# First stage with a fixed issue order and fp32 conditioning rows in column groups, and the second layer's output weights split early and kept in DRAM

## Chip, cores and metric

One core of one Trainium2 chip runs the whole program in one launch. The metric is the device time of an execution in microseconds (us); the median of several runs is compared.

## The reference, cut to what matters

Two layers over 2048 latent tokens of width 1024 and 256 context tokens. All arrays are fp32. Each layer computes

```python
shift, scale, gate = split(silu(c) @ w_mod + b_mod, 3)      # one row per stream (latent, context)
hx = rmsnorm(x, g_pre) * (1 + scale) + shift
q, k, v, ga, uf, gf, zc, bc, cc, gc = split_cols(hx @ w_in)
a = window_attention(rope(q), rope(k), v, kc, vc, sink)     # window 128 and 256 context keys
f = fourier_mix(uf, w_fourier)                              # 2-D FFT, then a 64x64 product per group
s = short_conv_mix(zc, bc, cc, conv_w, conv_b)
y = concat(a * silu(ga), f * silu(gf), s * silu(gc)) @ w_out
x = x + gate * rmsnorm(y, g_post)
```

The first product, `silu(c) @ w_mod`, is called the conditioning rows here: the columns for `shift` and `scale` of layer 0 (2048 of them, for the two streams) must be known before any token can be projected, and their weights are 8 MB.

## The kernel before

A large product is computed from two rounded parts of each operand: `split` (L76) writes `hi`, the fp32r rounding of the source, and `lo`, the rounded rest. It takes two letters, the engine for `hi` and the one for `lo`: v is VectorE, a ScalarE, p GpSimd. `proj_k` (L309) is then three matmuls, hi*hi, hi*lo and lo*hi, over 512 tokens. PE is TensorE.

Each layer has three parts: `half` (L782) for tokens 0 to 1023 and then for 1024 to 2047, each in two chunks of 512 tokens, projects all columns and writes q, k, v, the gates and the mixer inputs to DRAM; `phase2` (L1313) runs over blocks of 128 tokens: scores and softmax (`u_qk`, letter A), the product with the values (`u_pv`, B) and the output projection (`u_out`, C), interleaved by order strings such as `ORDER_1`. In `half` small generators ("fills") are advanced by `tick` after each `proj_k`, at a rate from `RT` or `FF`; a fill goes on at each yield.

Every DMA of the kernel is issued by SyncE (SP) in one queue, in order. The framework schedules the instructions of each engine in the order that its own planner finds, unless an instruction is kept in program order (`keep_in_program_order`) or put behind another (`issue_after`, in the kernel `behind`).

- `startup` (L652) is the first stage. It loads in the order of the string `LD` (g: a 512 KB tile of conditioning weights, x: 128 tokens of x, w: two tiles of projection weights, b: biases) and works in the order of `START`. `mod_mm(g)` (L685) makes a quarter of the conditioning rows: 8 weight slices of 128x512, each split in two (`MSH`, `MSL`), each part multiplied with a 4-column stationary operand (both streams, hi and lo), 16 matmuls for a quarter and 64 in all; then a copy, four transposes, a sum, and bias and gain. Letter m is one slice (the ninth m of a quarter its end), p one of eight `p0_post` steps (four transposes of x, scale and shift on ScalarE, split), W a weight split, 0 to 3 a `proj_k` of one of the four blocks of 128 columns, r the squares for chunk 1 (`pt_r`), y the steps of chunk 1 (`pt_row`, `pt_post`). A quarter serves two of the eight p steps. Chunk 1 of the same four blocks and the context tokens follow in `half` from L881 on, then `form_b` (L399).
- `tab_gen` (L612) is a fill of layer 0, half 0: it loads a piece of the FFT table, splits it (`a`, `v`) and stores it to `ftd`.
- `fft_b` (L543) is a fill of half 1 in both layers. Its tables come through `tab`, three buffers `ftb`. After the first split it yields four times before the first matmuls `pf`.
- `wout_gen` (L1280) makes the output weights in `phase2`: eight tiles of 512 KB are loaded and split there, in its first four steps (letters V and W of `ORDER_0` to `ORDER_3B`), into the four `big` buffers; those of W become free when the last `late` projection (L1054) is done.
- In `u_pv` (L1157) the half of the mixer output that doesn't come from attention (`fct`, by DMA) is split on GpSimd at the key tile t = 1 into `hfh` and `hfl`.

Of the kernel before, what the change touches and what calls it, by code (L numbers as in the profile page):

```python
# [16 lines left out]
DEPTH = 2  # L17
# [15 lines left out]
WE_B = ["vv", "vp", "vv", "av"]  # L33
WV_A = ["vv", "av", "vv", "vv"]
WV_B = ["vv", "av", "vv", "av"]
# [3 lines left out]
ORDER_3A = "bAAWCCBcBCABBAWCBBCBBCcACBCBB"  # L39
ORDER_3B = "bAAWCCBcBCABBAWCBBCBBCcACBCBB"  # L40
# [3 lines left out]
WST = ["ap", "av", "av", "vv"]  # L44
# [20 lines left out]
class Kern:  # L65
# [10 lines left out]
    def split(self, hi, lo, src, hi_eng="v", lo_eng="v"):  # L76
        nc = self.nc
        if hi_eng == "v":
            self.last_v = nc.vector.tensor_copy(hi, src)  # L79
        elif hi_eng == "a":  # L80
            nc.scalar.activation(hi, src, AF.Copy, bias=0.0, scale=1.0)  # L81
        else:
            nc.gpsimd.tensor_scalar(hi, src, 1.0, 1.0, op0=ALU.mult, op1=ALU.mult)  # L83
        if lo_eng == "v":
            self.last_v = nc.vector.tensor_tensor(lo, src, f(hi), op=ALU.subtract)  # L85
        else:
            nc.gpsimd.tensor_tensor(lo, src, f(hi), op=ALU.subtract)  # L87
# [136 lines left out]
    def p0_pre(self, l, base, n, ctx, xt, load=True, eng=None, sq=()):  # L224
# [14 lines left out]
        for i in range(nt):  # L239
            if eng and eng[i] == "p":  # L240
# [7 lines left out]
    def p0_post(self, l, ps, tag, xt, h, n, ctx, lo_eng="vpvpvpvp"):  # L248
# [4 lines left out]
        for k in range(KT):  # L253
            pt = ps.tile([128, CH], F32, name="pt", tag=tag)
            for i in range(n // 128):
                nc.tensor.transpose(pt[:, i * 128:(i + 1) * 128], xt[i][:, k * 128:(k + 1) * 128], self.ident)
            t = self.xp.tile([128, CH], F32, name="ht", tag="ht", bufs=2)
            nc.scalar.activation(t[:, :n], pt[:, :n], AF.Identity, bias=S[:, k, s:s + 1], scale=G[:, k, s:s + 1])
# [3 lines left out]
    def pt_r(self, slot, base, n, ctx, xt=None):  # L262
# [6 lines left out]
        for i in range(nt):  # L269
            jk = self.xp.tile([128, D], BF16, name="jk", tag="jk", bufs=1)  # L270
            self.last_sq = nc.scalar.activation(jk, xt[i], AF.Square, bias=0.0, scale=1.0,
                                                accum_out=ssq[:, i:i + 1])
# [9 lines left out]
    def pt_row(self, slot, n, ps, rb):  # L282
# [7 lines left out]
        nc.scalar.copy(rb, pb[:, :n])  # L290
        return rb

    def pt_post(self, T, h, n, ctx):
# [5 lines left out]
        for k in range(KT):  # L299
            u = self.xp.tile([128, CH], F32, name="ht", tag="ht", bufs=2)[:, :n]  # L300
            nc.vector.scalar_tensor_tensor(u, T[k], G[:, k, s:s + 1], rb, op0=ALU.mult, op1=ALU.mult)
            nc.scalar.activation(hi[:, k, :n], u, AF.Identity, bias=S[:, k, s:s + 1], scale=1.0)
            nc.vector.scalar_tensor_tensor(lo[:, k, :n], u, S[:, k, s:s + 1], f(hi[:, k, :n]), op0=ALU.add, op1=ALU.subtract)
# [5 lines left out]
    def proj_k(self, a, W, h, n, k):  # L309
# [3 lines left out]
        nc.tensor.matmul(a, wh[:, k, :], hi[:, k, :n], start=(k == 0), stop=False)  # L313
        nc.tensor.matmul(a, wh[:, k, :], lo[:, k, :n], start=False, stop=False)  # L314
        nc.tensor.matmul(a, wl[:, k, :], hi[:, k, :n], start=False, stop=(k == KT - 1))  # L315
# [227 lines left out]
    def fft_b(self, fp, ps, AB, ct):  # L543
# [42 lines left out]
        for _ in range(4):  # L586
            yield
# [24 lines left out]
    def tab_gen(self, p):  # L612
        nc = self.nc
        for k in range(9):
            raw = p.tile([128, 384], F32, name="tr", tag="tr")
            nc.sync.dma_start(raw, self.I["ftab"][:, k])
# [4 lines left out]
            yield  # L621
# [30 lines left out]
    def startup(self, ps, hx, blocks, st, wps, gps):  # L652
# [5 lines left out]
        slots = [t[:, i] for t in tmp for i in range(2)]  # L658
        slots += [st.tile([128, D], F32, name=n, tag=n) for n in ("cosT", "sinT")]
        slots += [gps.tile([128, D], F32, name=f"wmg{i}") for i in range(2)]  # L660
        wm = [big[k // 4][:, k % 4] for k in range(KT)] + slots

        def load(i):
            nc.sync.dma_start(wm[i], self.I["wmod0"][i])

        cs = gps.tile([128, KT, 4], F32R, name="cshl")
        self.split(cs[:, :, 0::2], cs[:, :, 1::2], self.cs, "v", "v")
        n = {"g": 0, "x": 0, "w": 0, "b": 0}
        for c in LD:
# [6 lines left out]
            elif c == "w":  # L676
                raws = [self.wraw(self.I["wina"][0, j]) for j, _ in blocks[:2]]
            else:
# [4 lines left out]
        post = self.p0_post(0, ps, "tr", x0, hx, CH, False)  # L683

        def mod_mm(g):  # L685
            pr = ps.tile([4, CH], F32, name="pmr", tag="fft")
            for k in range(KT):
                tags = (("qh", "ql"), ("rt", "rs"))[k % 2]
                hi, lo = [st.tile([128, CH], F32R, name=f"w{t}", tag=t, bufs=2) for t in tags]
                self.split(hi, lo, wm[4 * g + k // 2][:, k % 2 * CH:(k % 2 + 1) * CH], MSH[8 * g + k], MSL[8 * g + k])  # L690
                nc.tensor.matmul(pr, cs[:, k, :], hi, start=(k == 0), stop=False)
                nc.tensor.matmul(pr, cs[:, k, :], lo, start=False, stop=(k == KT - 1))
                yield
            row = st.tile([128, CH], F32, name="sg", tag="sg", bufs=2)[:4]
            nc.scalar.copy(row, pr)
            pc = ps.tile([128, 2, 2, 2, 2], F32, name="pmc", tag="fft")
            for n in range(2):
                for i in range(2):
                    o = (2 * n + i) * 128
                    nc.tensor.transpose(pc[:, n, i], row[:, o:o + 128], self.ident[:4, :4])  # L700
            sm = gps.tile([128, 2, 2, 2], F32, name="msum", tag="msum")
            nc.vector.tensor_reduce(sm, pc, axis=mybir.AxisListType.X, op=ALU.add)
# [845 lines left out]
```

## Time and profile before

| | us |
|---|---|
| median of 3 runs | 2036.09 (2033.15 to 2039.77) |
| profiled execution, device time | 2036.74 |
| its span in the profile | 2034.9 |
| PE busy in it | 1973.3 (97%) |
| VectorE / ScalarE / GpSimd busy | 1242.0 / 848.6 / 753.6 |

The span is the time from the first to the last recorded instruction; the device time is 1.8 us longer. A matmul's recorded duration is longer than its share of PE, since matmuls overlap: the distance of two starts is what one costs. "Idle before" is time in which the engine had nothing running, with the work that released it. Of the 40 slices of the span PE is at 6 tenths in the first, at 9 or more in the 38 after it, and at 8 in the last.

### The profile page before, as it was taken

How to read it: one execution, taken by the hardware profiler on the slowest of the kernel's cores; microseconds unless marked ns; L12 is line 12 of the kernel's file. 1: busy time of each engine (PE TensorE's matmuls, PEld its weight loads, DVE VectorE, ACT ScalarE, POOL GpSimd, SP SyncE). 2: the span in 40 equal slices, each digit the busy share in tenths (PEclk: the TensorE clock that was granted, in tenths of full speed). 3: DMA queues.
4: the chain of work that ended last, by engine and by line, in shares of the span. 5: the costliest groups of instructions: out<-in, count | busy, mean ns of one | idle time of the engine just before them, and what ended most of it. 6: DMA issues, size and time to landing. Idle time of an engine off the chain costs nothing. (4 is left out here: it accounts for less than half of the span.)

```text
span 2034.9 us, 28515 instructions
## 1 busy us (share of the span) xinstructions
PE 1973.3 (97%) x10232; PEld 1670.6 (82%) x10232; DVE 1242.0 (61%) x2239; ACT 848.6 (42%) x1742; POOL 753.6 (37%) x965
## 2 busy tenths in 40 slices
PE   6999999999999999999999999999999999999998
PEld 2898878897887788888877988889788778888886
DVE  7825695646525677777768323142754377777775
ACT  6522212313224556666666322131222356666663
POOL 4322212305342444444455233242234334444442
PEclk8999999999999999999999999999999999999999
DMA  7775654466467344443334533134554834444321
GB/s 298 226 250 158 206 185 141 142 199 186 158 168 218 96 112 115 114 115 104 127 122 137 164 96 94 62 119 132 156 168 141 239 109 116 114 116 113 110 63 42
DMA packets 187038, 291.63 MB, mean 143 GB/s; under 512 B 15608, under 2 KB 119696, under 8 KB 185872
## 3 DMA queue, kind: packets, MB, share of 16 engines
q1 hardware_dynamic: 186896, 289.80, 47.2%
q8 instruction: 81, 1.33, 0.3%
q14 instruction: 61, 0.50, 0.1%
HBM read 214.37 MB, written 75.38 MB: 142 GB/s over the span
## 5 line engine op out<-in xcount | busy, mean ns | idle before, releaser
L315 PE MATMUL acc<-big,wl 128*128 128x512 f32 x1152 | 452.4, 393 | 5.5 <-DVE wl L85 2.9
L313 PE MATMUL acc<-big,wh 128*128 128x512 f32 x1152 | 455.7, 396 | 1.4 <-DVE wh L79 1.4
L314 PE MATMUL acc<-big,wh 128*128 128x512 f32 x1152 | 451.3, 392 | 0.0
L87 POOL TENSOR_TENSOR wl<-wr,wh 128x1024 fp32r<-128x1024 f32 x63 | 162.9, 2586 | 377.4 <-ACT wh L81 234.9
L85 DVE TENSOR_TENSOR pl<-tp,ph 128x512 fp32r<-128x512 f32 x320 | 219.0, 687 | 105.6 <-ACT ph L81 101.2
L1141 ACT ACTIVATE pt<-pt,nm 128x640 f32<-128x640 f32 (+2 forms) x272 | 216.2, 795 | 130.2 <-DVE nm L1138 129.7
L315 PEld LDWEIGHTS acc<-big,wl 128*128 128x128 f32 x1152 | 217.9, 189 | 53.1 <-DVE wl L85 4.2
L313 PEld LDWEIGHTS acc<-big,wh 128*128 128x128 f32 x1152 | 218.5, 190 | 43.8 <-ACT czc L991 1.5
L314 PEld LDWEIGHTS acc<-big,wh 128*128 128x128 f32 x1152 | 218.1, 189 | 42.4 <-DVE big L85 0.2
L81 ACT ACTIVATE ph<-tp 128x512 fp32r<-128x512 f32 x320 | 188.8, 592 | 131.6 <-PE tp L1179 122.1
L1138 DVE CUSTOM_DVE_ANT_0 pt<-sp,mask,nsink 128x640 f32<-128x640 f32 (+2 forms) x256 | 213.3, 841 | 20.7 <-PE sp L1128 15.0
L1153 POOL TENSOR_SCALAR pt<-pt,rv 128x640 f32<-128x640 f32 (+2 forms) x272 | 213.2, 804 | 26.9 <-DVE rv L1151 26.1
L1179 PE MATMUL tp<-ident,pt 128*128 128x128 f32 x1280 | 197.1, 275 | 10.1 <-POOL pt L1153 9.5
L1179 PEld LDWEIGHTS tp<-ident,pt 128*128 128x128 f32 x1280 | 160.1, 141 | 56.8 <-POOL pt L1153 15.3
L358 POOL TENSOR_TENSOR rs<-rs,sinT 128x512 f32<-128x512 f32 x40 | 66.0, 1653 | 170.0 <-DVE rs L356 165.2
L1131 PE MATMUL sp<-kseg,qt 128*128 128x384 f32 (+1 forms) x512 | 128.6, 331 | 0.0
L1228 PE MATMUL yp<-big,hfh 128*128 128x512 f32 x272 | 118.7, 436 | 1.0 <-POOL hfh L83 1.0
L1146 POOL TENSOR_TENSOR es<-nm,nsink 128x4 f32<-128x4 f32 x68 | 14.5, 214 | 283.2 <-DVE nm L1138 283.2
L1228 PE MATMUL yp<-big,hah 128*128 128x512 f32 x272 | 117.1, 431 | 0.1
L1128 PE MATMUL sp<-kctx,qt 128*128 128x256 f32 x544 | 114.2, 292 | 2.9 <-DVE nm L1138 2.0
L1128 PEld LDWEIGHTS sp<-kctx,qt 128*128 128x128 f32 x544 | 95.6, 189 | 16.4 <-DVE nm L1138 3.5
L1230 PE MATMUL yp<-big,hfl 128*128 128x512 f32 x272 | 108.1, 397 | 0.5 <-POOL hfl L87 0.4
(382 smaller groups left out, 3807.9 us busy)
## 6 DMA issues: line engine op xcount, KB each, us to landing
wr<-in_wina SPq DMA_DIRECT2D x76, 512.0 KB, 3.6
qt<-qs SPq DMA_DIRECT2D x34, 512.0 KB, 4.7
wmt<-in_wmodt SPq DMA_DIRECT2D x32, 512.0 KB, 4.3
ftb<-ftd SPq DMA_DIRECT2D x36, 384.0 KB, 3.7
xt<-in_x SPq DMA_DIRECT2D x26, 512.0 KB, 5.8
kseg<-ks SPq DMA_DIRECT2D x24, 512.0 KB, 7.9
xt<-x SPq DMA_DIRECT2D x24, 512.0 KB, 5.1
gat<-gas SPq DMA_DIRECT2D x34, 256.0 KB, 3.1
```

The lines of the kernel that those rows point to most:

```text
L81: nc.scalar.activation(hi, src, AF.Copy, bias=0.0, scale=1.0)
L85: self.last_v = nc.vector.tensor_tensor(lo, src, f(hi), op=ALU.subtract)
L87: nc.gpsimd.tensor_tensor(lo, src, f(hi), op=ALU.subtract)
L313: nc.tensor.matmul(a, wh[:, k, :], hi[:, k, :n], start=(k == 0), stop=False)
L314: nc.tensor.matmul(a, wh[:, k, :], lo[:, k, :n], start=False, stop=False)
L315: nc.tensor.matmul(a, wl[:, k, :], hi[:, k, :n], start=False, stop=(k == KT - 1))
L1128: nc.tensor.matmul(sp[:, 256:512], B.q[:, h, :], self.kctx[:, kv, x, :], start=(x == 0), stop=(x == 1))
L1138: self.last_m = nc.vector.tensor_tensor_reduce(d, x, m, scale=-0.125, scalar=self.nsink[:, h:h + 1], op0=ALU.add, op1=ALU.min, accum_out=n ...
L1141: self.last_x = nc.scalar.activation(pt, pt, AF.Exp, bias=nm[:, hh:hh + 1], scale=-1.0, accum_out=sm[:, hh:hh + 1])
L1153: self.last_p = nc.gpsimd.tensor_scalar(B.pts[kv][g], B.pts[kv][g], rv[:, g:g + 1], 1.0, op0=ALU.mult, op1=ALU.mult)
L1179: nc.tensor.transpose(tp[:, hh * 128:(hh + 1) * 128], pts[hh][:, t * 128:(t + 1) * 128], self.ident)
L1228: nc.tensor.matmul(yp, hh, wh[:, k, :], start=(i == 0), stop=False)
```

## The change

1. First stage. Every instruction of it goes through `self.kp`, which keeps it in program order while `START` runs. The conditioning weights are no longer split: a slice is one fp32 matmul with a 32-column stationary operand (two columns are used), and slices k go in turn to the four column groups 0, 32, 64 and 96, whose results lie in four groups of 32 rows and are summed after the transposes. A step m is now two slices, and a quarter has five steps. `LD`, `START` and the engines of several small steps are new: x is loaded first, all four weight blocks and the x of chunk 1 in the same queue; nine steps i at the start are four transposes of the identity each; the scaling of x goes from GpSimd to ScalarE and VectorE, the low parts of p from half GpSimd to all VectorE, all four W to ScalarE and VectorE.
2. Layer 1's output weights are split by a new fill, `wout_split`, in half 0 of layer 1 (16 pieces of 128x512) and stored to DRAM (`wos`); `phase2` of layer 1 loads both parts, twice the bytes, with no split there. The first block of a layer splits `fct` at its last key tile (of layer 0's first block this is t = 1 as before).
3. `tab_gen` loads a piece ahead, and `fft_b` yields once, not four times, after its first split.
4. Evacuations of chunk 0 are put behind the copy of the row factors (`last_rb`), the context's row factors are made one k later, and `form_b_w` of later halves is put behind `last_v`.

```diff
-LD = "gggxgxxxgggwbggggggggg"
-XE = "pppv"
-START = "mmmmmmmmmmmWmpp0m1mm1m00mp1pmm0mmmW123p32mmmmp0m1m2m13m03mm2rmm3pp102y23y001213yyyyy01y23"
+LD = "xxxxgbgggwcggggggggggggX"
+XE = "avav"
+START = "iiiiiiiiimmmmWmpp00W11WWmmmmm2233ppmmmm00m112233ppmmmm00mr1122pp330011y2233yzyyy"
-RT = 0.6, 0.594, 0.616, 0.1, 0.15, 0.12, 0.49, 0.16
+RT = 0.6, 0.594, 0.616, 0.1, 0.15, 0.12, 0.49, 0.16, 0.27
+ORDER_2B = "bAACACACCCBCBCBCBABBCBBB"
+ORDER_3B = "bWAAWCCBcBCABBAWCBBCBBCcACBWCBB"
...
         def mod_mm(g):
-            pr = ps.tile([4, CH], F32, name="pmr", tag="fft")
+            pr = ps.tile([128, CH], F32, name="pmr", tag="fft")
             for k in range(KT):
-                tags = (("qh", "ql"), ("rt", "rs"))[k % 2]
-                hi, lo = [st.tile([128, CH], F32R, name=f"w{t}", tag=t, bufs=2) for t in tags]
-                self.split(hi, lo, wm[4 * g + k // 2][:, k % 2 * CH:(k % 2 + 1) * CH], MSH[8 * g + k], MSL[8 * g + k])
-                nc.tensor.matmul(pr, cs[:, k, :], hi, start=(k == 0), stop=False)
-                nc.tensor.matmul(pr, cs[:, k, :], lo, start=False, stop=(k == KT - 1))
-                yield
+                q = 32 * (k % 4)
+                self.kp(nc.tensor.matmul(pr[q:q + 32], cs[:, k, :], wm[4 * g + k // 2][k % 2],
+                                         start=(k < 4), stop=(k >= 4), tile_position=(0, q)))
+                if k % 2:
+                    yield
...
+            elif c == "i":
+                w = ps.tile([128, CH], F32, name="warm", tag="tr")
+                for i in range(4):
+                    self.kp(nc.tensor.transpose(w[:, i * 128:(i + 1) * 128], self.ident, self.ident))
...
         h = part(0)
-        for _ in range(4):
-            yield
+        yield
...
+        raw = load(0)
         for k in range(9):
-            raw = p.tile([128, 384], F32, name="tr", tag="tr")
-            nc.sync.dma_start(raw, self.I["ftab"][:, k])
+            yield
+            nx = load(k + 1) if k < 8 else None
             yield
...
+            elif half == 0:
+                fills.append(self.start_fill(self.wout_split(l, self.pool(e3, "wop", bufs=1)), RT[8]))
...
-            if kv == 1 and t == 1:
+            if kv == 1 and t == (1 if B is not self.Bs[0] else nkt - 1):
...
+    def wout_load(self, l, n):
+        W = [self.big(), self.big()]
+        self.wout.append(W)
+        for c in (2, 3, 0, 1):
+            with self.behind(self.last_st):
+                for t, src in zip(W, self.wos[n]):
+                    self.nc.sync.dma_start(f(t[:, 2 * c:2 * c + 2]), src[:, 2 * c:2 * c + 2])
+            yield
+
+    def wout_split(self, l, p):
+        nc = self.nc
+
+        def load(i):
+            t = p.tile([128, CH], F32, name="wo", tag="wo", bufs=2)
+            nc.sync.dma_start(t, self.I["woutk"][l, i // KT, :, i % KT])
+            return t
+
+        raw = load(0)
+        for i in range(2 * KT):
+            yield
+            nx = load(i + 1) if i + 1 < 2 * KT else None
+            yield
+            h = p.tile([128, 2, CH], F32R, name="wh2", tag="wh2", bufs=2)
+            self.split(h[:, 0], h[:, 1], raw, "a", "v")
+            nc.sync.dma_start(self.wos[i // KT, :, :, i % KT].rearrange("x p c -> p x c"), f(h))
+            raw = nx
+        yield
```

## Rows read from the trace of the kernel before

**Rows 1.** Busy time in stretches of 50 us: PE, PEld, DVE, ACT, POOL, clock, DMA.
```profile
250.00:300.00 50.00, 46.09 (x231) 39.02 (x230) 42.85 (x73) 8.42 (x16) 11.72 (x5) 0.97 0.65 216
...
450.00:500.00 50.00, 45.66 (x213) 37.86 (x213) 36.95 (x80) 14.39 (x25) 22.27 (x14) 0.97 0.56 156
...
1450.00:1500.00 50.00, 45.83 (x227) 38.72 (x226) 31.35 (x52) 16.47 (x30) 25.76 (x18) 0.97 0.75 205
...
1600.00:1650.00 50.00, 45.38 (x233) 37.04 (x232) 35.85 (x61) 25.31 (x53) 17.86 (x21) 0.97 0.62 200
...
sum 2050.00, PE 1973.31 PEld 1670.56 DVE 1241.95 ACT 848.59 POOL 753.55; mean PE 48.13 PEld 40.75 DVE 30.29 ACT 20.70 POOL 18.38
```

**Rows 2.** PE in order of time, 0 to 40 us: start, duration, idle before.
```profile
6.08 0.59 PE L691 MATMUL pmr<-wqh,cshl 128*4 128x512 f32 x1 [6.08 <-ACT wqh L81]
...
21.11 0.48 PE L256 MATMUL pt<-ident,xt 128*128 128x128 f32 x1 [3.71 <-POOL xt L241]
```

**Rows 3.** Groups by line, 0 to 62 us: busy us, mean ns, idle before.
```profile
L691 PE MATMUL pmr<-wqh,cshl 128*4 128x512 f32 x16 | 7.4, 461 | 8.4 <-ACT wqh L81 8.4
...
L271 ACT ACTIVATE jk<-xq 128x1024 bf16<-128x1024 f32 x4 | 4.2, 1054 | 0.1
...
L695 ACT COPY sg<-pmr 4x512 f32<-4x512 f32 x4 | 2.3, 572 | 1.8 <-PE pmr L692 1.7
```

**Rows 4.** Busy time in stretches of 10 us; clock, DMA share and GB/s last.
```profile
0.00:10.00 10.00, 3.67 (x8) 0.55 (x9) 3.31 (x7) 5.32 (x9) 1.82 (x6) 1.00 0.71 277
10.00:20.00 10.00, 3.58 (x14) 0.88 (x12) 2.80 (x6) 8.04 (x15) 4.45 (x8) 0.84 1.02 409
20.00:30.00 10.00, 7.63 (x23) 3.63 (x24) 10.00 (x15) 4.85 (x7) 7.90 (x4) 0.50 1.04 404
30.00:40.00 10.00, 8.50 (x41) 4.93 (x40) 9.15 (x19) 6.57 (x13) 3.48 (x3) 0.98 0.98 390
```

**Rows 5.** PE in order of time, 60 to 93 us.
```profile
60.44 0.60 PE L256 MATMUL pt<-ident,xt 128*128 128x128 f32 x4
60.79 0.48 PE L313 MATMUL acc<-big,wh 128*128 128x512 f32 x1
...
82.75 0.30 PE L289 MATMUL prb<-ident,ht 128*128 128x128 f32 x1 [1.69 <-DVE ht L288]
...
92.57 0.39 PE L315 MATMUL acc<-big,wpl 128*128 128x512 f32 x1
92.80 0.28 PE L313 MATMUL acc<-cxh,wh 128*128 128x256 f32 x1
```

**Rows 6.** PE in order of time, 146 to 148 us: four fp32 products, then a projection.
```profile
146.34 1.05 PE L437 MATMUL pa<-wf,cf 128*128 128x128 f32 x8
147.15 0.48 PE L313 MATMUL acc<-big,wh 128*128 128x512 f32 x1
```

**Rows 7.** VectorE, then PE, in order of time, 288 to 294 us.
```profile
288.51 0.56 DVE L85 TENSOR_TENSOR th<-tr,th 128x384 fp32r<-128x384 f32 x1 [1.54 <-ACT th L81]
...
293.58 0.80 PE L315 MATMUL acc<-big,wl 128*128 128x512 f32 x1 [2.54 <-POOL wl L87]
```

**Rows 8.** SP's queue, then PE, in order of time, 480 to 487 us.
```profile
482.34 0.59 SPq L343 DMA_DIRECT2D qs<-ql  x1
483.03 1.02 SPq L555 DMA_DIRECT2D ftb<-ftd  x2
...
486.38 0.98 PE L428 MATMUL pf<-ftb,fh 128*128 128x256 f32 x6 [3.09 <-DMA ftb<-ftd]
```

**Rows 9.** GpSimd, VectorE and PE in order of time, 1613 to 1642 us.
```profile
1613.52 0.62 POOL L83 TENSOR_SCALAR hfh<-fct 128x512 fp32r<-128x512 f32 x1 [3.07 <-DMA fct<-fs]
...
1637.31 3.23 POOL L87 TENSOR_TENSOR big<-wr,big 128x1024 fp32r<-128x1024 f32 x1 [1.29 <-PE tp L1179]
...
1638.23 2.87 DVE L1070 SCALAR_TENSOR_TENSOR lt<-ht,lt 128x512 f32<-128x512 f32 x1
...
1641.75 0.80 PE L1193 MATMUL op<-pl,vtl 128*128 128x512 f32 x1 [2.24 <-DVE pl L85]
```

More of the change, by code (lines that the diff above doesn't have):

```diff
@@ L289, in pt_row @@
             nc.tensor.transpose(pb[:, sl], w[:, sl], self.ident)
-        nc.scalar.copy(rb, pb[:, :n])
+        self.last_rb = nc.scalar.copy(rb, pb[:, :n])
         return rb
@@ L657, in startup @@
         tmp = [t.rearrange("p k c -> p (k c)").rearrange("p (h c) -> p h c", h=2) for t in tmp]
[L658 to L661, printed above, removed]
-        def load(i):
[L664 to L668, printed above, removed]
+        wm = [big[k // 4][:, k % 4] for k in range(KT)] + [t[:, i] for t in tmp for i in range(2)]
+        wm = [[w[:, i * CH:(i + 1) * CH] for i in range(2)] for w in wm]
+        wm += [[st.tile([128, CH], F32, name=f"w{t}{i}", tag=t, bufs=2) for i in range(2)] for t in ("qh", "ql")]
+        slots = [gps.tile([128, D], F32, name=f"wmg{i}") for i in range(2)]
+        wm += [[w[:, i * CH:(i + 1) * CH] for i in range(2)] for w in slots]
+        craw = [st.tile([128, KT, 128], F32, name=n, tag=n) for n in ("cosT", "sinT")]
+        def load(i):
+            if 12 <= i < 14:
+                for h in range(2):
+                    nc.sync.dma_start(wm[i][h], self.I["wmod0"][i][:, h * CH:(h + 1) * CH])
+            else:
+                t = slots[i - 14] if i >= 14 else (big[i // 4][:, i % 4] if i < 8 else tmp[(i - 8) // 2][:, i % 2])
+                nc.sync.dma_start(t, self.I["wmod0"][i])
+        cs = gps.tile([128, KT, 32], F32, name="cs32")
+        nc.vector.memset(cs, 0.0)
+        nc.vector.tensor_copy(cs[:, :, 0:2], self.cs)
+        n = dict.fromkeys("gxwbcX", 0)
         for c in LD:
@@ L677, in startup @@
                 raws = [self.wraw(self.I["wina"][0, j]) for j, _ in blocks[:2]]
+            elif c == "c":
+                for t, (j, _) in zip(craw, blocks[2:]):
+                    nc.sync.dma_start(t, self.I["wina"][0, j].rearrange("p (k c) -> p k c", k=KT))
+            elif c == "X":
+                self.p0_load(0, CH, CH, False, self.x1)
             else:
@@ L876, in half @@
             if first:
-                self.pt_r(2, 0, NCTX, True, self.xs)
                 _, n, ctx, tok, rp = chunks[0]
-                for (j, ev), acc in zip(blocks0, accs):
-                    ev(acc, n, ctx, tok, rp)
+                with self.behind(self.last_rb):
+                    for (j, ev), acc in zip(blocks0, accs):
+                        ev(acc, n, ctx, tok, rp)
                 h, n, ctx, tok, rp = chunks[1]
@@ L889, in half @@
                         self.proj_k(accs[i], Ws0[i], h, n, k)
-                        if i == 2 and k:
+                        if i == 2 and k > 1:
                             next(pc)
+                            if 4 < k < 7:
+                                next(pc)
                             if k == KT - 1:
@@ L923, in half @@
                 fetch(J_K)
-                WB = self.form_b_w(l, wb)
+                with self.behind(self.last_v):
+                    WB = self.form_b_w(l, wb)
                 if l == 0:
```

108 lines of the change are left out of this document (56 added, 52 removed).

## The prediction

> **What bounds the kernel now.** I read the busy time in stretches of 50 us first. PE is busy for 1973 of 2035 us [rows 1], and its work hardly changes, so a change can gain only what PE loses: 61.6 us without work, and stretches at half clock. The stretches show where. The first 40 us hold 16.6 us of idle PE (6.3, 6.4, 2.4 and 1.5 in turn), with a clock of 0.50, the 1.2 GHz level, from 20 to 30 us [rows 4]. Four later stretches hold 3.9, 4.3, 4.2 and 4.6 us, each with a mean clock of 0.97 [rows 1]; 0.97 over 50 us is 3 us at half clock, so some 1.5 us more is lost in each.
>
> Then the order of time on PE. The first matmul starts at 6.08 us, released by a ScalarE rounding of conditioning weights, and at 21.11 PE stands 3.71 us for GpSimd, which scales x [rows 2]. By line, the first matmul of a slice, hi, waits 8.4 us in all for ScalarE's rounding [rows 3]: the splits feed PE too slowly, while DMA runs at full share and some 400 GB/s [rows 4]. From 60 us on PE is dense but for 1.69 us at 82.75; a projection matmul starts every 0.23 us, and chunk 1 ends at 92.80 us [rows 5]. Chunk 1 is 96 matmuls, at 0.228 us 21.9 us; with the gap it began at 92.8 - 21.9 - 1.7 = 69.2 us. This 69.2 is what the first stage has to beat.
>
> **The change part by part.**
>
> *Conditioning rows.* Removed: 64 matmuls at 0.23, 14.7 us of PE at full clock, and 64 split instructions on three engines. Added: 32 fp32 matmuls of 512 columns. No row shows one in a column group. The nearest are four fp32 products of 128 columns at full width: eight records in 0.81 us (146.34 to 147.15) [rows 6], so each is two records of 0.10 us, 0.203 us in all. Scaled to 512 columns that is 0.81 us, two records of 0.4. Bounds: 0.81 us each with no overlap between column groups, 26 us in all; a quarter of it, 0.2, if four groups run together, 6.5 us. I take the middle, 0.41: the two records of one product use the same columns and cannot overlap, and matmuls start in order, so the first record of the next group can overlap only with the second of the last. That is 13 us, about what is removed. So the gain here is not PE work: it is that nothing stands between a landed tile and its matmul.
>
> The Trainium skill, "TensorE: Matmul & The Clock Gate", Part 3, has three column groups of 32 running 2.38 times as fast as one after the other; no row here shows that. By it the 32 would cost 26/2.38 = 11 us, 2 us less than my sum; with four groups wholly together it is the second case below. "TensorEngine Tiling", Key Properties, speaks against the change: switching the tiling mode drains the engine. The order string switches eight times; with a drain taken as a matmul's recorded 0.39 less its distance of 0.23 [rows 5], that estimate is 1.3 us.
>
> *The first stage anew.* Transfers: x (2.1 MB), 16 conditioning tiles (8.4) and four weight blocks (2.1) come in one queue; 2.8 MB land by 10 us, then about 0.405 MB per us [rows 4]. So quarter 1 is complete after 8.4 MB, at 10 + 5.6/0.405 = 23.9 us, and the last quarter after 12.6 MB, at 34.2. By 23.9 PE can have done quarter 0 and blocks 0 and 1 for k = 0 and 1. After it, in the pinned order, PE has: the last step of quarter 1 and two quarters more, 18 matmuls at 0.41 = 7.4 us; 84 projection matmuls at 0.228 = 19.2 us; six p steps at 0.35 (60.44 to 60.79 [rows 5]) = 2.1 us; three groups of four transposes, 1.1 us. Sum 29.8 us, to 53.7. Waits on top: the end of quarter 1 stands behind its copy of 0.57 us [rows 3], some 0.7 us with the hand-over, and the four pinned squares of 1.05 us plus their reads [rows 3] stand on ScalarE ahead of the scaling of the last two p steps: up to 2 us, I take 1. The x of chunk 1 lands after 14.7 MB, at 39.5, in time for those squares. So chunk 0 ends near 55.5, and 2.5 us more go until chunk 1 has its row factors (four transposes, 0.35 [rows 5], a copy, 0.57 [rows 3], and a VectorE and a ScalarE step over 512 columns, taken as the copy and a little more). Chunk 1 starts near 58 in place of 69.2: 11 us. If the 1.69 us at 82.75 goes too, since its step comes a k later, it is 13; I take **12**. Bounds: 0.2 per fp32 matmul saves 3.8 us, gain 16; 0.81 costs 7.2 plus a delay of quarter 0 of 3, gain 2. What is added elsewhere is covered: VectorE gets four weight splits and four low parts, but loses the 32 low parts that filled it to 10.00 and 9.15 of 10 us [rows 4]. GpSimd's scaling leaves the path altogether. The warm-up transposes run before the first tile has landed, while PE stood until 6.08 anyway [rows 2]; they cost nothing unless they last past 9 us.
>
> *tab_gen.* At 288.51 VectorE stands 1.54 us behind ScalarE's part of a table piece whose load was issued just before; the weight split queued behind is late, and PE loses 2.54 at 293.58 and 1.37 before [rows 7], the 3.9 us of [rows 1], plus 1.5 of clock. With the load two yields earlier the head of the queue is ready. Gain 0 to 5.4; I take **4**, since the named wait goes and the rest is 1 us of other lateness.
>
> *fft_b.* The table loads for the second group were issued at 483.03 behind stores of q which wait for their own split, and PE stood 3.09 us for them [rows 8]; with a wait just before it is 4.3 us here and 4.2 in layer 1 [rows 1], with the clock 11.5 in both. Three yields fewer move the first matmuls some 3.5 us up (a yield is 1.7 ticks at the rate 0.58, a tick 0.68 us), so the loads may come ahead of one batch of stores, but then the group that needs them is earlier too. Gain 0 to 11.5; I take **5**, the middle.
>
> *Output weights in DRAM.* In half 0 of layer 1 16 splits of 128x512 and 12.6 MB of transfers are added, under PE that is busy there; SP also gets 32 issues in that queue, whose stores wait for VectorE's low part with loads behind them: 0 to 2 us, I take 1. In `phase2` layer 1 the eight splits go; the stretch has 4.6 us of idle PE and 1.5 of clock [rows 1]. At 1638.23 a VectorE step over 512 columns takes 2.87, just while GpSimd splits weights for 3.23, and PE loses 2.24 [rows 9]. At 1613.52 GpSimd's queue stands 3.07 us for `fct` [rows 9], which the later split of the first block avoids; the attention steps queued behind are on time. Against this, the loads are 8.4 MB in place of 4.2. The second 4.2 MB can begin only when their buffers are free, near 1636, and need 10 us at 400 GB/s or 21 at the 200 of that stretch [rows 1]; `u_out` for them begins about a step and a half later, near 1656, so it is just covered. What is late next would be the loads of q and keys, behind the weights in SP's queue. Gain 0 to 6; I take **4**, less the 1 above: **3**.
>
> Sum: 12 + 4 + 5 + 3 = 24 us. Against the profiled 2036.7 (which is 0.6 above the median, well inside the runs' spread) that is **2012.5 us**.
>
> **The rivals.** *Four groups run together.* The order pinned on PE is for overlapping matmuls; against it, no row shows any. Then 16 in place of 12: **2008**. *Queues keep the stalls.* SP and ScalarE remain in order, and the stall is one of order, not of size [rows 8]; then tab_gen and fft_b give 1 of 9: **2020.5**. *No overlap.* Each fp32 matmul costs 0.81; the start gives 2: **2022.5**. *Both of the last two*: 24 - 8 - 10 = 6 us, **2031**, which is no change. *Slower: the thin matmuls run one by one at the low clock.* In the stage as it is PE held only half clock from 20 to 30 us while busy for 7.6 of 10 [rows 4]. If that holds in the new stage, the 24 fp32 matmuls of quarters 1 to 3 cost 1.62 each, 39 in place of 10; chunk 1 starts near 87 instead of 58, 18 us later than now, and with the 12 of the other parts the time is **2043**. From 0.9 us per fp32 matmul on (12/24 above 0.41) the stage loses, and from 1.4 on the whole is slower. Against it: the waits that broke PE's work up there (8.4 us in [rows 3]) are the ones removed.
>
> **How the numbers follow.** My case has 0.43, four groups 0.18, stalls kept 0.12, no overlap 0.12, both 0.08, slower 0.07. The predicted time is that of the first, with a range of its own from 2004 to 2020. The full range reaches down past the four groups with all stalls gone (16 + 5 + 11 + 6 = 38, 1998) and up past the no-overlap case, to 2029; it leaves out the last two cases and a little below. A change of 0.3%, 6 us, is what can be told from none. Faster 0.85 (the first four), same 0.08, slower 0.07.
>
> **What would show it.** Chunk 1's first matmul near 58 us and the context projection near 80, not 92.8; fp32 conditioning matmuls starting some 0.4 us apart for a product (0.2: together; 0.8: none); no PE wait for ScalarE's rounding; clock at full from 20 us. No idle PE at 290 us less the shift, nor where the second group of `pf` waits for `ftb`. In layer 1's `phase2` PE idle under 2 us in the first 50, and no wait for a weight tile. The prediction is wrong if PE, pinned, waits for ScalarE or VectorE in the first stage for more than 5 us, if the fp32 matmuls start 0.8 us apart or more, or if what the stage gains comes back as a wait in the context projection or `form_b`, where VectorE's work follows closely.

## The result and the profile after

| | before | after |
|---|---|---|
| median of the runs compared, us | 2035.25 (4 runs) | 2014.6 (4 runs, 2013.59 to 2022.6) |
| ratio, 95% interval | | 0.9898 [0.9883, 0.9914] |
| profiled execution, device time | 2036.74 | 2014.54 |
| its span | 2034.9 | 2012.5 |
| PE / VectorE / ScalarE / GpSimd busy | 1973.3 / 1242.0 / 848.6 / 753.6 | 1963.7 / 1221.1 / 839.9 / 714.0 |

The change takes 20.7 us off; 24 were forecast (2012.5), and the measured time is inside the range. The total came out nearly right while its terms did not: the first stage gave half of what I had put down for it, and the output weights gave nearly four times as much. PE's idle time falls from 61.6 to 48.8 us, and its mean granted clock over the profiled execution rises from 0.989 to 0.993.

To see where time comes from I take the start of the same PE matmul in both profiles (the same one counted from the end; times from the start of each span) and subtract: the lead. It is 12.4 us at the last matmul of chunk 0 (68.67 and 56.25 us), 8.1 at the first of chunk 1 (68.89 and 60.83) and 6.2 at the context projection (92.80 and 86.60). Then it is 6.3 at 300 us, 10.5 at 400, 9.4 at 590, 10.8 at 1120, 5.2 at 1160, 7.0 at 1400, 11.5 at 1590 and 22.5 from 1670 on. So the time is gained in steps, and some of it is lost again: half of the first step up to the context projection, and 6 us at 1135 us.

The stretches of the changed kernel, in the columns of [rows 4] and [rows 1]: busy time of PE, PEld, DVE, ACT and POOL, clock, DMA share, GB/s.

```profile
0.00:10.00 10.00, 6.53 (x36) 6.29 (x36) 0.51 (x3) 4.97 (x9) 0.19 (x4) 1.00 0.77 269
10.00:20.00 10.00, 5.74 (x28) 1.90 (x28) 3.49 (x10) 5.28 (x7) 2.02 (x6) 1.00 1.03 407
20.00:30.00 10.00, 8.11 (x41) 4.64 (x42) 6.44 (x14) 4.44 (x6) 0.00 (x0) 1.00 1.03 407
30.00:40.00 10.00, 10.00 (x60) 6.96 (x59) 3.04 (x11) 2.04 (x3) 0.00 (x0) 1.00 1.00 392
...
60.00:70.00 10.00, 8.89 (x31) 6.97 (x32) 9.20 (x14) 4.64 (x10) 5.14 (x8) 0.83 0.64 210
80.00:90.00 10.00, 9.74 (x55) 8.37 (x54) 9.56 (x19) 8.94 (x20) 2.03 (x1) 1.00 0.84 292
...
250.00:300.00 50.00, 47.38 (x238) 40.13 (x238) 42.92 (x81) 6.65 (x13) 10.18 (x5) 0.97 0.50 168
450.00:500.00 50.00, 45.82 (x226) 38.67 (x225) 38.20 (x68) 17.10 (x30) 27.95 (x18) 0.97 0.69 195
1450.00:1500.00 50.00, 49.13 (x249) 41.83 (x248) 28.44 (x46) 15.60 (x30) 25.99 (x18) 1.00 0.74 223
1600.00:1650.00 50.00, 50.00 (x281) 42.54 (x280) 32.97 (x67) 30.87 (x68) 20.09 (x32) 1.00 0.83 256
1650.00:1700.00 50.00, 50.00 (x283) 42.93 (x282) 38.17 (x74) 30.48 (x68) 21.82 (x44) 1.00 0.41 111
```

The last of these stretches in the kernel before:

```profile
1650.00:1700.00 50.00, 48.14 (x260) 40.51 (x259) 36.02 (x69) 29.98 (x67) 22.62 (x42) 0.97 0.30 81
```

Against [rows 4], the clock in this profile no longer falls from 20 to 30 us, and ScalarE's roundings are gone from PE's waits. Against [rows 1], the stretch at 1450 now has under 1 us without PE work and those at 1600 and 1650 none, all at full clock; the one at 250 lost 1.3 of its 3.9 us, the one at 450 nothing.

PE of the changed kernel in order of time: start, duration, idle before and its releaser.

```profile
2.70 6.53 PE L746 MATMUL warm<-ident 128*128 128x128 f32 x36 [2.70 <-DMA ident<-in_ident]
11.44 1.05 PE L709 MATMUL pmr<-big,cs 128*32 128x512 f32 x4 [2.21 <-DMA big<-in_wmod]
...
18.13 0.66 PE L719 MATMUL pmc<-ident,sg 128*128 128x128 f32 x4 [1.78 <-ACT sg L714]
20.86 0.50 PE L313 MATMUL acc<-big,wh 128*128 128x512 f32 x1 [1.20 <-DVE big L77]
24.90 1.92 PE L709 MATMUL pmr<-big,cs 128*32 128x512 f32 x16
...
60.83 0.50 PE L313 MATMUL acc<-big,wh 128*128 128x512 f32 x1 [3.85 <-ACT big L301]
75.85 0.30 PE L288 MATMUL prb<-ident,ht 128*128 128x128 f32 x1 [1.22 <-DVE ht L287]
86.60 0.28 PE L313 MATMUL acc<-cxh,wh 128*128 128x256 f32 x1
...
284.64 0.47 PE L313 MATMUL acc<-big,wh 128*128 128x512 f32 x1 [0.80 <-DVE mo L188]
287.17 0.51 PE L315 MATMUL acc<-big,wl 128*128 128x512 f32 x1 [1.82 <-POOL wl L85]
470.30 0.74 PE L428 MATMUL pm__4165<-PQ,AB 128*128 128x256 f32 x4 [2.12 <-DVE PQ L83]
1135.34 0.69 PE L411 MATMUL accb<-wbh,big 128*128 128x384 f32 x1 [3.62 <-DVE ql L83]
```

At 24.90 eight fp32 products, 16 records, take 1.92 us: 0.24 for a product. (The single records start in four rounds 0.43 us apart, the four of a round within 0.02 us; by the distance of starts a product costs 0.21.) Chunk 1 starts at 60.83, not 58, after 3.85 us without work. The context projection starts at 86.60, where [rows 5] have 92.80 and I expected 80. The 1.69 us of [rows 5] is still there as 1.22 at 75.85.

### The profile page after: what moved, and what is told of

It reads as the page before. It is cut to its first block, busy times and chain, and to the rows that moved or that the text cites. A ratio compares the mean times of both kernels' runs of the same rounds, so it can differ in the third digit from the quotient of the medians.

```text
span 2012.5 us, 28555 instructions
## 1 busy us (share of the span) xinstructions
PE 1963.7 (98%) x10268; PEld 1672.2 (83%) x10268; DVE 1221.1 (61%) x2221; ACT 839.9 (42%) x1726; POOL 714.0 (35%) x951
## 5 line engine op out<-in xcount | busy, mean ns | idle before, releaser
L85 POOL TENSOR_TENSOR wl<-wr,wh 128x1024 fp32r<-128x1024 f32 x62 | 155.4, 2507 | 385.8 <-ACT wh L79 255.1
L1178 POOL TENSOR_SCALAR pt<-pt,rv 128x640 f32<-128x640 f32 (+2 forms) x272 | 208.7, 785 | 24.2 <-DVE rv L1176 23.4
L193 DVE CUSTOM_DVE_ANT_0 jk<-wmt,sb 128x1024 bf16<-128x1024 f32 x56 | 81.0, 1446 | 45.8 <-DMA wmt<-in_wmodt 45.2
```

The costliest lines, as they stand in the source:

```text
L1178: self.last_p = nc.gpsimd.tensor_scalar(B.pts[kv][g], B.pts[kv][g], rv[:, g:g + 1], 1.0, op0=ALU.mult, op1=ALU.mult)
```

## Experiments

Each was run beside the kernel before on the same chip; the ratio is to that. The distance from the changed kernel is the difference of the ratios by 2036 us; the two intervals together make it uncertain by 4 to 6 us, and by 7.5 in the run marked *. So it is clear of noise for four kernels alone: weights split in phase 2, one column group, four yields, and first stage only.

| kernel | median, us | ratio, 95% interval | from the changed kernel, us |
|---|---|---|---|
| weights split in phase 2 again | 2027.47 | 0.9953 [0.9937, 0.9969] | +11.2 |
| one column group | 2029.66 | 0.9971 [0.9959, 0.9983] | +14.9 |
| no warm-up transposes | 2016.01 | 0.9905 [0.9886, 0.9923] | +1.4 |
| context's squares last | 2012.74 | 0.9883 [0.9867, 0.9900] | -3.1 |
| row factors first * | 2014.92 | 0.9913 [0.9880, 0.9947] | +3.1 |
| x of half 1 behind the gate | 2011.89 | 0.9892 [0.9867, 0.9916] | -1.2 |
| four yields in fft_b | 2021.23 | 0.9932 [0.9912, 0.9952] | +6.9 |
| old tab_gen | 2017.78 | 0.9909 [0.9889, 0.9930] | +2.2 |
| form_b's weights free | 2015.75 | 0.9897 [0.9879, 0.9915] | -0.2 |
| first stage only | 2030.12 | 0.9970 [0.9958, 0.9983] | +14.7 |
| row factors first, low part on GpSimd, x behind | 2015.11 | 0.9903 [0.9884, 0.9923] | +1.0 |
| context's squares last, x behind | 2009.74 | 0.9880 [0.9862, 0.9898] | -3.7 |

One part needed no run. With the split of `fct` put back to t = 1 everywhere, the program has the same instructions, in the same order and with the same waits, on every engine: this part of the change does nothing.

**Fp32 products in one column group.**

```diff
-                q = 32 * (k % 4)
-                self.kp(nc.tensor.matmul(pr[q:q + 32], cs[:, k, :], ..., start=(k < 4), stop=(k >= 4), tile_position=(0, q)))
+                self.kp(nc.tensor.matmul(pr[0:32], cs[:, k, :], ..., start=(k == 0), stop=(k == KT - 1), tile_position=(0, 0)))
...
```

The copy and the transposes behind it are narrowed to these 32 rows, and a copy takes the place of the sum over groups.

> The changed kernel, but all eight fp32 products of a quarter go into column group 0 (32 rows of PSUM, accumulated there), so that no two can overlap. Theory (four column groups run together, 0.22 us per product against some 0.81 alone): products start 0.7 to 0.85 us apart, chunk 0 ends 10 to 16 us later, and most of it stays to the end: 2022 to 2030. Rival (the stage is bound by the arrival of the weights and by the chain to chunk 1, so PE has room): products as slow, but the time within 4 us of the changed kernel.

PE of this kernel, in the columns above:

```profile
25.38 7.05 PE L708 MATMUL pmr<-big,cs 128*32 128x512 f32 x16
...
76.75 0.80 PE L313 MATMUL acc<-big,wh 128*128 128x512 f32 x1 [3.85 <-ACT big L301]
```

The same eight products take 7.05 us, 0.88 each, 3.7 times the 0.24 of four groups: the groups run together. Here the single records start 0.43 us apart, one after the other, so a product costs 0.86 by the distance of starts, four times the 0.21. Chunk 1 starts 15.9 us later and the program ends 14.9 us later, so the stage has no room to hide them. With products one after the other this stage would have been slower than before (the lead at the context projection is -9.7 us), not 2 us faster as I had it.

**No warm-up transposes.**

```diff
-START = "iiiiiiiiimmmmWmpp00W11WW...
+START = "mmmmWmpp00W11WW...
```

> The changed kernel without the 36 transposes of the identity at the start. Theory (they only fill time before the first tile has landed; the clock in the first 60 us is held by the work itself): the same time within 2 us. Rival (without them the clock falls to its lower level in the first 30 us, and the stage loses 3 us or more): 2018 or more, with PEclk under 0.9 between 10 and 30 us.

The stretch from 20 to 30 us, first of this kernel, then of the one with x behind the gate, which has the transposes:

```profile
20.00:30.00 10.00, 8.65 (x38) 4.68 (x39) 6.26 (x14) 3.89 (x5) 0.00 (x0) 0.83 1.03 407
```

```profile
20.00:30.00 10.00, 7.91 (x34) 4.43 (x35) 5.77 (x9) 4.66 (x6) 0.00 (x0) 0.83 1.03 406
```

The clock is 0.83 here, but also in three of the twelve profiles of kernels with the transposes; 1.4 us is within the interval, and the context projection starts 0.8 us later than in the changed kernel (87.41). That they save time is not shown, nor that the clock from 20 us on needs them.

They do raise the clock earlier. In the changed kernel they start 0.21 us apart up to 7.45 us and 0.11 from 7.65 on, and the two rounds of the first tile start 0.42 us apart (11.45 and 11.87), where without the transposes it is 0.82 (10.71 and 11.54). (The 1.00 of the first stretch is the mean of what is recorded of the clock in it, which begins at 7.6 us; the transposes' distances show the lower level until then.) But in both kernels PE begins a new pair of products only every 1.28 us there, the pace at which the tiles land, so little of it reaches the time.

**The context's squares last, and the row factors first.** In the changed kernel ScalarE sets the start of chunk 1; its order there:

```profile
57.01 0.59 ACT L289 COPY rb<-prb 128x512 f32<-128x512 f32 x1 [7.64 <-PE prb L288]
57.49 1.06 ACT L271 ACTIVATE jk<-xc 128x1024 bf16<-128x1024 f32 x1
...
58.54 0.59 ACT L816 ACTIVATE sg<-acc 128x512 f32<-128x512 f32 x1
59.02 1.06 ACT L271 ACTIVATE jk<-xc 128x1024 bf16<-128x1024 f32 x1
...
60.05 0.72 ACT L301 ACTIVATE big<-ht,mo 128x512 fp32r<-128x512 f32 x1
```

Two squares for the context and an evacuation stand between the row factors' copy and the first hi part of chunk 1, which PE awaits.

```diff
-START = ...pp330011y2233yzyyy"
+START = ...pp330011y2233yyyyz"      (context's squares last)
+START = ...pp3300y11y2233yyyz"      (row factors first)
```

> The changed kernel with the two squares of the context tokens (letter z) last in the pinned order, behind the fourth step of chunk 1 instead of ahead of its second. Theory (chunk 1 begins at 60.8 us, 3.9 us after PE is out of work, because these squares of 1.05 us each stand on ScalarE ahead of the first hi part): chunk 1 begins 1.5 to 3 us earlier, the half clock from 62 to 65 us shrinks, and the time falls by 2 to 5 us, to 2010 to 2012.5. Rival (VectorE, busy 9 of 10 us from 60 to 90, sets the pace of chunk 1): it begins earlier but ends as late, within 1 us of the changed kernel.

> The changed kernel with the order string's end changed: the transposes of chunk 1's row factors and the first step of chunk 1 come ahead of the last projections of blocks 1 to 3 of chunk 0, and the context's squares (z) last. Theory (the 3.9 us that PE stands ahead of chunk 1 are the chain row factors, copy, u, hi; once this chain runs under chunk 0's last matmuls the stand goes): idle ahead of chunk 1 under 1 us, no half clock from 62 to 65 us, and 2 to 4 us less than with z last alone, 2008.5 to 2011. Rival (VectorE, busy 9 of 10 us from 60 to 90, sets when chunk 1 ends): chunk 1 begins 2 us earlier than with z last alone, ends within 0.7 us of it, and the time is the same within 1 us.

With the squares last chunk 1 starts at 59.58 after 2.27 us of idle PE, and the context projection at 83.67, 2.9 us earlier than in the changed kernel. At the end of the profile 1.8 us of that is left; by the ratio it is 3.1, inside the interval, so that the gain stays is likely and not shown. With the row factors first PE has no idle time ahead of chunk 1, and the context projection starts at 82.79. But then, VectorE and PE of this kernel:

```profile
83.94 2.50 DVE L83 TENSOR_TENSOR wbl<-wr,wbh 128x768 fp32r<-128x768 f32 x1
86.36 0.87 DVE L302 SCALAR_TENSOR_TENSOR cxl<-ht,mo,cxh 128x256 fp32r<-128x256 f32 x2
...
86.89 0.39 PE L314 MATMUL acc<-cxl,wh 128*128 128x256 f32 x1 [1.70 <-DVE cxl L302]
```

A split of the next step's weights runs ahead of the context's last low parts, and PE waits for those. It takes 2.50 us beside a subtraction on GpSimd (83.51 to 85.62); in the changed kernel the same step takes 0.96, after GpSimd is done:

```profile
88.20 0.96 DVE L83 TENSOR_TENSOR wbl<-wr,wbh 128x768 fp32r<-128x768 f32 x1
```

The lead over the changed kernel falls from 3.9 us at 70 to 1.7 at 110; the time shows no gain. That is the rival, VectorE sets the end, with GpSimd holding VectorE up.

**Work taken off VectorE.**

```diff
-SPB = 'pvpp', 'pppp'
+SPB = 'pppp', 'pppp'
```

With this the low part goes to GpSimd; the row factors are first and x of half 1 behind the gate (below).

> Three edits on the changed kernel: the order string of the run with the row factors ahead of chunk 0's end; the one low part of form_b's weights that VectorE rounded in the first half (2.50 us at 83.94 in that run, ahead of the last low parts of the context, for which PE stood 1.70 us at 86.89) on GpSimd, which is idle from 70 to 80 us; and x of layer 1's second half behind the last gate. Theory (from 60 to 90 us VectorE, busy 9 to 10 of 10 us, sets when the first stage is through, so only work taken off VectorE keeps what an earlier chunk 1 gains): no PE wait over 1 us in the context projection, and 5 to 8 us less than the changed kernel, 2007 to 2010. Rival (the first stage's gain is lost later anyway, near 290 and 480 us, by queues that catch up): like the run with x behind alone, 2011 to 2013.

VectorE, GpSimd and PE of this kernel:

```profile
82.36 3.89 DVE L302 SCALAR_TENSOR_TENSOR cxl<-ht,mo,cxh 128x256 fp32r<-128x256 f32 x2
...
81.90 4.07 POOL L85 TENSOR_TENSOR wbl<-wr,wbh 128x768 fp32r<-128x768 f32 x2 [11.02 <-DVE wbh L77]
...
84.33 0.39 PE L314 MATMUL acc<-cxl,wh 128*128 128x256 f32 x1 [0.75 <-DVE cxl L302]
86.30 0.56 PE L314 MATMUL acc<-cxl,wh 128*128 128x256 f32 x1 [1.34 <-DVE cxl L302]
```

The theory fell. Two low parts that take 0.87 us in the run before took 3.89 and ended at 86.25, 0.28 us after GpSimd's two subtractions: VectorE does not run them beside GpSimd. The lead drops from 11.6 at 80 us to 8.0 at 110. Taking work off VectorE and giving it to GpSimd took nothing off the path.

**The wait at 1135 us.** VectorE and GpSimd of the changed kernel ahead of it:

```profile
1125.13 1.41 DVE L243 TENSOR_SCALAR xt<-xt,rr 128x1024 f32<-128x1024 f32 x2 [2.31 <-POOL rr L117]
...
1128.36 0.74 DVE L243 TENSOR_SCALAR xt<-xt,rr 128x1024 f32<-128x1024 f32 x1
...
1131.27 2.30 DVE L359 TENSOR_TENSOR rt<-rt,rs 128x512 f32<-128x512 f32 x1 [0.47 <-DVE rt L357]
...
1130.21 2.81 POOL L85 TENSOR_TENSOR wl<-wr,wh 128x1024 fp32r<-128x1024 f32 x1
```

Four scalings of x, for layer 1's second half, stand ahead of the rotation of the current block; and the rotation's sum takes 2.30 us beside GpSimd's weight split, where it takes 0.69 alone. The accumulator that PE needs comes free 3.62 us late.

```diff
-                    self.p0_pre(l, HALF, CH, False, x0)
+                    with self.behind(self.last_g):
+                        self.p0_pre(l, HALF, CH, False, x0)
```

> The changed kernel, but the loads, squares and scalings of x for layer 1's second half are put behind the last gate of its first half, so that they no longer stand on VectorE ahead of the evacuation of the first key and query blocks of layer 1. Theory (these four scalings at 1125 to 1129 us delay the shuffle, so the rotation and the rounding of q, and PE waits 3.62 us for a free accumulator at 1135.34 and then runs at half clock to 1140.6): the wait is under 1 us, the lead over the kernel before no longer falls by 6 us between 1120 and 1160, and the time is 2009 to 2012. Rival (the chain is late from the rotation and the weight split on GpSimd alone): the wait stays over 2.5 us and the time stays within 1.5 us of the changed kernel.

PE has no wait from 1120 to 1150 us, and the lead there grows by 6 us against the changed kernel. The median is 2.7 us lower; by the ratio it is 1.2, not outside the interval. So the wait needs the scalings ahead of the rotation, but they do not make it alone: with the squares last VectorE does the same there at the same time (four scalings from 1125.47, a sum of 2.33 us), PE comes 3 us later and waits 0.94; and with form_b's weights free (below) the scalings stand there and PE does not wait. What the wait is worth in time is not shown.

**The four yields, the old tab_gen, and form_b's weights.** Each is that part undone.

```diff
-        yield
+        for _ in range(4):
+            yield
```
```diff
-            t = p.tile([128, 384], F32, name="tr", tag="tr", bufs=2)
+            t = p.tile([128, 384], F32, name="tr", tag="tr")
...
-        raw = load(0)
         for k in range(9):
-            yield
-            nx = load(k + 1) if k < 8 else None
+            raw = load(k)
             yield
...
-            raw = nx
-        yield
+            yield
```
```diff
-                with self.behind(self.last_v):
-                    WB = self.form_b_w(l, wb)
+                WB = self.form_b_w(l, wb)
```

> The changed kernel with the four yields of fft_b restored, in both layers. Theory (the earlier first matmuls gained the table wait of the second group in layer 1, 5 us in the lead between 1390 and 1490 us, and nothing in layer 0): 2018 to 2021, with a wait of 2 us or more for ftb again in layer 1. Rival (the waits went because the other edits moved the queues, the yields do nothing): within 1.5 us of the changed kernel.

> The changed kernel with tab_gen as before: one buffer, a load just ahead of its split. Theory (the load ahead took the 2.5 us wait at 290 us and about 4 us at the site near 389 us): 2018 to 2020, with PE waits of over 2 us near 282 to 290 us. Rival (one wait only takes the place of the other, what is gained at 290 is 1.5 us): 2015 to 2017.

> The changed kernel with form_b's weights of the later halves no longer put behind the last VectorE split. Theory (this part, costed at nothing, does nothing: the kernels without the fills' changes and the one with the first stage alone leave no more than 1 us for it): within 2 us of the changed kernel, PE waits at 1135 us as there. Rival (it is what took the 2.03 us wait near 389 us, which none of the other runs that keep it shows, and which the run with the first stage alone still has): that wait is back and the time is 2018 to 2020.

PE with four yields, with the old tab_gen, and with form_b's weights free, in this order:

```profile
474.63 0.50 PE L428 MATMUL pm__4180<-PQ,AB 128*128 128x256 f32 x2 [4.25 <-ACT PQ L79]
480.56 1.65 PE L428 MATMUL pf<-ftb,fh 128*128 128x256 f32 x6 [2.58 <-DMA ftb<-ftd]
...
1467.45 0.98 PE L428 MATMUL pf<-ftb,fh 128*128 128x256 f32 x6 [3.09 <-DMA ftb<-ftd]
```

```profile
285.94 0.47 PE L313 MATMUL acc<-big,wh 128*128 128x512 f32 x1 [2.07 <-DVE wh L77]
289.18 0.80 PE L315 MATMUL acc<-big,wl 128*128 128x512 f32 x1 [2.54 <-POOL wl L85]
```

```profile
382.69 0.50 PE L315 MATMUL acc<-big,wl 128*128 128x512 f32 x1 [2.33 <-DVE wl L83]
```

The yields are worth 6.9 us. In layer 0 the wait for `ftb` of [rows 8] comes back (2.58 us, with 4.25 just before it), while the changed kernel has shorter ones in their place (2.12 at 470.30, and 1.27 for `ftb` at 555.26); in layer 1 it is 3.09 where the changed kernel waits 0.99 at 1537.48. Against the changed kernel 3.6 us of lead go between 440 and 590 us and 3.7 between 1400 and 1590. So the theory held, but layer 0 gained as much as layer 1.

The old tab_gen brings back the 2.54 us of [rows 7]. The changed kernel's row at 284.64 names the conditioning sums (`mo`, L188), but that matmul reads `wh`, which VectorE rounds just before them:

```profile
283.81 0.69 DVE L77 CAST wh<-wr 128x1024 fp32r<-128x1024 f32 x1
```

So with the new tab_gen PE still waits there for the same weight split, 0.80 us for its hi part and 1.82 for GpSimd's low part, in place of 2.07 and 2.54: over half of the wait is left. The time does not show what the rest is worth: 2.2 us is inside the interval, and in the one profile of the old tab_gen the lead is 3.1 us less than the changed kernel's at 300 us and 1.2 more at the end.

Form_b's place was costed at nothing, and its time is nothing. But its trace is not the same: without it the wait near 385 us is back, 2.33 us, and the one at 1135 us is gone. The changed kernel trades one for the other, and so does every profile: the three kernels without this part (the one before, the first stage alone and this one) wait 1.7 to 2.3 us near 385 and not over 0.7 at 1135; the other eleven do not wait over 0.7 near 385, and the eight of them with x unmoved wait 0.9 to 3.8 us near 1135 (1150 with one column group).

**The output weights split in phase 2 again, and the first stage alone.** The first takes the order strings and the engines of the splits of the kernel before with it. The second undoes the three parts of the section above as well, so that only the first stage is new.

```diff
...
-            elif half == 0:
+            elif 0:
...
-            wgen = self.wout_load if l else self.wout_gen
+            wgen = self.wout_gen
...
-                    emit(gens, (ORDER_0, ORDER_1, (ORDER_2, ORDER_2B)[l], (ORDER_3, ORDER_3B)[l])[s])
+                    emit(gens, (ORDER_0, ORDER_1, ORDER_2, ORDER_3)[s])
```

> The changed kernel (2014.6 us), but layer 1's output weights are loaded and split in phase 2 as in the kernel before, and the fill wout_split is left out; the later split of fct stays. Theory (the splits in phase 2 and the queue slots they took carry the 11 us by which phase 2 of layer 1 became shorter): 2022 to 2026, with PE idle 3 to 5 us again around 1570 to 1620 us. Rival (the later split of fct on GpSimd and another order around it carry most): at most 2018. If the fill costs PE time in half 0 of layer 1, its start shows a lead over the changed kernel before phase 2.

> Only the new first stage: tab_gen, fft_b, the output weights of layer 1 and form_b's place are as in the kernel before. Theory (the first stage leads by 6 us at the context projection and nothing behind it undoes that; the stall at 1135 us comes with another part): 2029 to 2031, and no wait over 1 us near 1135. Rival (the earlier start is given back by the waits of the later stages, at 290, 480 and 1135 us, so that the other parts make up all of the 21 us): 2033 to 2037.

VectorE, GpSimd and PE of the first of them, and its stretch from 1600 us:

```profile
1625.98 2.86 DVE L1097 SCALAR_TENSOR_TENSOR lt<-ht,lt 128x512 f32<-128x512 f32 x1
...
1625.06 3.23 POOL L87 TENSOR_TENSOR big<-wr,big 128x1024 fp32r<-128x1024 f32 x1 [1.28 <-PE tp L1206]
...
1629.50 0.49 PE L1220 MATMUL op<-pl,vtl 128*128 128x512 f32 x1 [2.23 <-DVE pl L85]
...
1600.00:1650.00 50.00, 43.75 (x234) 34.94 (x233) 40.52 (x69) 28.11 (x60) 22.88 (x28) 1.00 0.55 164
```

That is the picture of [rows 9], and the splits in phase 2, with the order that goes with them, cost 11.2 us by the ratio. By the lead they cost 8.2: at 1590 us it is the changed kernel's (11.7 and 11.5), and at the end 14.3 in place of 22.5. Of the 8.2, 6.3 us is idle time of PE in one stretch, at full clock. No cost of the fill shows before phase 2.

The first stage alone gives 6.1 us (1 - 0.9970 of 2036), near its lead of 5.6 us at 90 us, and has no wait at 1135. That nothing behind it undoes the lead does not hold in its profile: the lead is 5.4 at 400 us, 2.2 at 590, 1.3 at 1120 and 3.9 at the end. That execution took 2032.88 us, 2.8 over the median.

**Squares last and x behind.** The edits of those two runs together.

> The changed kernel with the context's squares last in the pinned order and x of layer 1's second half behind the last gate. Theory (the two gains of 2.5 and 3.3 us are at places 1050 us apart and add up): 2008.5 to 2010.5. Rival (what is gained before is lost at the waits for queues near 290, 480 and 560 us): 2011 to 2013.

2009.74 us is the lowest median of all, 0.9880 [0.9862, 0.9898] of the kernel before. Its interval overlaps the changed kernel's, so it beats the kernel before, and the changed one probably, which is not shown.

## Why the prediction was right, and where its steps were off

- *Conditioning rows.* 0.41 us per product was the middle of the bounds; measured 0.24, nearly the lower one (0.21 by the distance of starts). The step that failed is "the two records of one product use the same columns and cannot overlap, and matmuls start in order, so the first record of the next group can overlap only with the second of the last": the first records of four groups start together, and their second records 0.43 us later. The Trainium skill, "TensorE: Matmul & The Clock Gate", Part 3, has 2.38 for three groups; these four fp32 groups gave 3.7. The 1.3 us estimated for the eight switches of the tiling mode was somewhat high: from a projection to the first product it is 0.32 us (24.585 to 24.903) where two projections are 0.23 apart, and back at a projection some 0.2 us are lost (33.112 to 33.634 and 33.971, 0.52 and 0.34 in place of 0.43 and 0.23); with the switches that lie inside a wait it is under 1 us in all.
- *The first stage, 12 us; measured 6.1.* Three sizes were off. Chunk 0's last matmul started at 56.25, near the 55.5, though the products cost half: at 24.90 all eight products of quarter 1 were still to do, where I had its last step, because PE had waited 1.78 us for quarter 0's copy and 1.20 for VectorE's rounding of x. The chain to chunk 1 took 4.6 us, not 2.5: I had the squares of chunk 1 in the sum, but not those of the context, pinned ahead of its first hi part. So chunk 1 started 8.1 us earlier, not 11. And it took 25.8 us, where it took 23.9 before and I had it shorter: "What is added elsewhere is covered" was read off the VectorE stretches up to 40 us, and in 60 to 90 us VectorE is busy 9 to 10 of 10. That the pace is not PE's own shows in the nine profiles with this order behind the transposes of the identity: chunk 1 takes 25.7 to 25.8 us in all, whether PE is idle for 1.5 us of it and at half clock for 3.4, or 0.5 and 5.7. With the squares last it takes 24.1, so ScalarE's part of the chain counts too. By the prediction's own sign this stage went wrong: PE waits for ScalarE or VectorE sum to 8.4 us up to the start of chunk 1, where over 5 was named.
- *tab_gen, 4 us; measured 2.2,* which the interval does not tell from nothing. VectorE's stand for ScalarE's part of the table piece went, but the weight split behind it is still late: the step that failed is "the named wait goes", since 2.62 us of it is left.
- *fft_b, 5 us; measured 6.9,* right in mechanism, in both layers, and in size within the interval.
- *Output weights in DRAM, 3 us; measured 11.2, or 8.2 by the lead.* The mechanism was named: VectorE and PE late beside GpSimd's split [rows 9]. The term was mis-sized: I counted idle time and clock of one stretch of 50 us, took two thirds, and subtracted 1 us for the fill, which costs nothing that the lead shows. Before the change the waits run on into a second such stretch, also at a mean clock of 0.97; the two hold 6.5 us of idle PE, and after the change none. "The later split of the first block" was no change at all. The loads of twice the bytes were covered, as forecast.
- *Costed at nothing.* Form_b's place removes about 4 us of lead loss at 385 and brings the wait at 1135.

The parts measured by themselves add up to 6.1 + 2.2 + 6.9 + 11.2 = 26.4 us; the whole gave 20.7. The two cannot be told apart, since each part is uncertain by 2.5 to 5 us. The wait at 1135 us, 6 us of lead, is of the size of the difference and stands in the kernel with all parts, but neither in the first stage alone nor with form_b's weights free; without it the time was the same, so that it is the difference is not shown. The total was close by luck: the first stage, 6 us too high, and the weights, 8 us too low, nearly cancelled. Of the rivals, "four groups run together" was true in its mechanism, but its 2008 was not, since the stage ended on the chain through ScalarE and VectorE and not on PE.

## What to carry to other kernels

When PE gets its operands sooner, sum up what the engine behind it must do in the same stretch: here ScalarE and VectorE could follow only part of the way, and of the 12.4 us of lead at the end of chunk 0, 6.2 were left at the context projection. When a wait goes, look at which instructions stand ahead on each queue of the chain: moving two squares and one group of loads gave the lowest median, while products at half the assumed price did not end chunk 0 earlier than forecast. A split moved off a stretch where VectorE and GpSimd hold each other up can be worth much more than the one wait on PE that shows it (2.24 us in [rows 9], 8 to 11 us in all).

## What the runs showed of the hardware

Four column groups of fp32 products run 3.7 times as fast as one (1.92 against 7.05 us for eight), and four times by the distance of starts (0.21 against 0.86 us).

Two-input instructions of VectorE took longer while GpSimd worked on SBUF: 3.89 us in place of 0.87, 2.30 in place of 0.69, each ending 0.3 to 0.6 us after GpSimd's. The Trainium skill, "SBUF — State Buffer", Who interferes with whom, says that such a pair doesn't run at once and that the later one waits for the end of the earlier. These rows agree, and by that rule the low part moved to GpSimd holds VectorE's next low parts up for its own length. A rounding with one input stood as well: in the changed kernel `wbh` takes 2.22 us beside GpSimd's subtraction (85.72 to 87.75), and 0.55 at 91.43 with the row factors first.

```profile
85.95 2.22 DVE L77 CAST wbh<-wr 128x768 fp32r<-128x768 f32 x1
```

A wait has different lengths in executions whose instructions stand in the same order there: PE's wait near 285 us for `wh` was 0.80 us in the changed kernel and 2.26 in the one with x behind, which differs only from 1100 us on; that at 1135 us was 3.62 in the changed kernel and 0.94 with the squares last. One profile of each kernel is thus not enough to price a wait of a few us.
